# A hybrid encoder block on one Trainium2 core: a tenth gate and up pair of each FFN as a Strassen group, and half of each group's first sums made by an accumulating transfer

## The chip, the cores and the metric

The kernel runs on one core of one Trainium2 chip. The metric is device time in microseconds (us) of one execution. The engines named here are PE (TensorE, matrix products), DVE (VectorE), ACT (ScalarE), POOL (GpSimd, which here mostly issues transfers) and SP (SyncE, which issues the loads of raw weights).

## The reference, cut to what matters

One encoder block on 256 rows of width 2048, in float32: a half-step SwiGLU FFN, two token mixers (band attention and retention) whose outputs are gated and merged, a second FFN, and a final norm.

```
def swiglu_ffn(x, w_gate, w_up, w_down):          # 2048 -> 5632 -> 2048
    return (jax.nn.silu(x @ w_gate) * (x @ w_up)) @ w_down

x = x + 0.5 * swiglu_ffn(rmsnorm(x, norm_ffn1_g), ffn1_w_gate, ffn1_w_up, ffn1_w_down)
proj = rmsnorm(x, norm_mix_g) @ w_in              # q, k, v twice, three gates
...                                               # attention, retention
x = x + (sigmoid(gate_a) * (att @ w_out_att) + sigmoid(gate_r) * (ret @ w_out_ret)) @ w_out
x = x + 0.5 * swiglu_ffn(rmsnorm(x, norm_ffn2_g), ffn2_w_gate, ffn2_w_up, ffn2_w_down)
return rmsnorm(x, norm_final_g)
```

## The kernel before

**Products.** Every float32 product is made as three matmuls: weights and activations are split into a rounded part `hi` and the rest `lo`, and hi x hi, hi x lo and lo x hi are added up in PSUM (`three`, lines 131 to 133). A weight tile of 256 rows by 512 columns (512 KB) is split by one ACT cast (L123) and one DVE subtraction (L124) (`split`). Up to four split tiles exist at a time (`SPLIT_BUFS`), so splits run a few steps ahead of PE.

**Steps.** The whole program is one list of steps, and each step is one split tile and its products. A *standard* step loads its tile with an SP transfer into one of five raw buffers, and makes 12 matmuls (two 128-row tiles of rows, two chunks of K, three products). In this document it is written S.

**Strassen groups.** Gate and up of one 512-column block of an FFN (and pairs of columns of `w_in`) can be computed together as a 2 x 2 block product with seven instead of eight products (`class Strassen`). A group is named z with the number of its first step: z89 is the group that starts at step 89. It has 28 steps of 6 matmuls in four phases, each over four K chunks j = 0 to 3: r0 to r3 and s0 to s3 in phases 0, 1 and 2, and s0 to s3 alone in phase 3. Each group owns four tiles k (`kept`, loaded from up) and four tiles x (loaded from gate), which POOL loads (L507), in the order k0, x0, k1, x1, k2, x2, k3, x3. Then:
- Phase 0: r splits k. DVE adds k to x, the *first sum* (`first`, L496). s splits x.
- Phase 1: r splits a raw tile, which DVE then adds to x (L551). s splits x; then DVE makes k = x - k (L538), and POOL issues a transfer that adds a weight tile from DRAM to x, the *third sum* (`third`, L539).
- Phase 2: r splits a raw tile, s splits k. Phase 3: s splits x. After that the buffers go to later groups.

The order in which steps are prepared within a phase is r0 r1, s0 r2, s1 r3, s2 s3. In phase 0, r2's preparation holds the sum of x2, ahead of the split of s1.

**Order.** `weave` lays the groups one after another and puts standard steps between their pairs of steps. `SHARE` has one weight for each of the 16 pairs or single steps of a group; a credit grows by rate x weight, and when it is large enough, the next standard step of the queue is placed. A standard step of a down projection can only be placed when the blocks of its pass are at hand (`needs`, `makes`). `PLAIN` lists the blocks whose gate and up stay standard steps, and `PASSES` the groups of blocks that one pass over the down weights takes. Before, nine of the eleven blocks of each FFN are groups, and five more groups lie in the `w_in` product: 23 groups in all. POOL's queue holds the loads and third-sum transfers in the order of the program; the loads of the next group stand behind the third sums of the current one.

Of the kernel before, what the change touches and what calls it, by code (L numbers as in the profile page):

```python
# [11 lines left out]
ALU = mybir.AluOpType  # L12
# [28 lines left out]
RET_WAIT = (14, 5)  # L41
HELD = 6

SHARE = (0.85,) * 4 + (1.0,) * 4 + (0.8,) + (0.4,) * 3 + (0.15,) * 4
PLAIN = (9, 10)
PASSES = ((9, 0), (1, 2), (10, 3), (4, 5), (6,), (7,), (8,))
GATE_WAIT = 5
WARM = (6, 3)
TAIL_PARTS = ((0, slice(0, NB)), (1, slice(0, NB // 2)), (1, slice(NB // 2, NB)))

# [22 lines left out]
def block_kernel(ctx: ExitStack, tc: tile.TileContext, x, g1, w1g, w1u, w1d, gm, w_in, rel, woa, wor, wo,  # L73
                 g2, w2g, w2u, w2d, gf, cos, sin, decay, ident, out):
    nc = tc.nc
# [33 lines left out]
    def weights_tile(name):  # L109
        return wpool.tile([P, KC, NB], F32, tag="raw", bufs=RAW_BUFS, name=name)  # L110

    def chunk(w, r0, c0):
        return w[r0 : r0 + KC * P, c0 : c0 + NB].rearrange("(k p) n -> p k n", p=P)
# [367 lines left out]
    class Strassen:  # L481
# [20 lines left out]
        def loads(self):  # L502


            def go(tiles, i, jc):
                tiles[jc] = apool.tile([P, KC, NB], F32, tag="act", name=f"{self.name}{'kx'[i]}{jc}")
                nc.gpsimd.dma_start(tiles[jc], chunk(self.w[i], self.rows(0, jc), self.col[i]))  # L507

            return [
                lambda tiles=tiles, i=i, jc=jc: go(tiles, i, jc)  # L510
                for jc in range(HALF_K // KC) for i, tiles in enumerate((self.kept, self.x))
            ]
# [12 lines left out]
        def step(self, phase, jc, of_sum):  # L525
            made = {}
            name = f"{self.name}{phase}{jc}{'rs'[of_sum]}"
            n = HALF_K // KC

            def load():  # L530
                made["raw"] = weights_tile(f"raw{name}")
                i = 2 - phase
                fetch(made["raw"], self.w[i], self.rows(1, jc), self.col[i])

            def third():

                x, k = self.x[jc], self.kept[jc]
                nc.vector.tensor_sub(k, x, k)  # L538
                nc.gpsimd.dma_start(x, chunk(self.w[0], self.rows(1, jc), self.col[0]), accum_op=ALU.add)  # L539

            def prep():
                x = self.x[jc]
                if not of_sum:
                    if phase == 0:
                        made["w"] = split(self.kept[jc], name)
                        self.first(jc)
                        return
                    raw = made.pop("raw")
                    made["w"] = split(raw, name)
                    if phase == 1:  # L550
                        nc.vector.tensor_add(x, x, raw)  # L551
                elif phase == 2:
                    made["w"] = split(self.kept.pop(jc), name)
                elif phase == 3:
                    made["w"] = split(self.x.pop(jc), name)
                else:
                    made["w"] = split(x, name)
                    if phase == 1:
                        third()

            bank, form, fresh, closing = {
# [4 lines left out]
            }[phase, of_sum]  # L566

            def products():
                hi, lo = made["w"]
                if fresh and jc == 0:  # L570
                    self.bank(bank)
                for i in range(KC):
                    three(
                        self.acc[bank], self.norm.form(form, KC * jc + i), (hi[:, i, :], lo[:, i, :]),
                        fresh and jc == 0 and i == 0, closing and jc == n - 1 and i == KC - 1, True,
                    )
                if jc == n - 1:
                    self.end(phase, of_sum)

            loaded = not of_sum and phase in (1, 2)  # L580
            frees = ["raw"] if loaded else ["kept"] if of_sum and phase > 1 else []
            return Step(self, 0, load if loaded else None, prep, frees, products)
# [53 lines left out]
    def weave(jobs, apart, groups, lead, start=None):  # L636
# [18 lines left out]
        for _ in range(lead):  # L655
            next_standard()
        rate = (len(queue) - apart) / (len(groups) * sum(SHARE))
        credit = 0.0
        first = len(steps) - 8
        for n, (b, make) in enumerate(groups.items()):  # L660
# [5 lines left out]
            for i, part in enumerate(group.steps()):  # L666
                steps.extend(part)
                credit += rate * SHARE[i]
                if i + 1 == len(SHARE):
                    at_hand[b] = len(steps) + 6  # L670
# [5 lines left out]
    def ffn(name, norm, wg, wu, wd, after, start=None):  # L676


        nblocks = DFF // NB
        mids, ready = {}, {}  # L680

        def put_mid(b, hs):
            mids[b] = Operand(f"{name}a{b}", 1)
            for t in range(NT):
                mids[b].put(0, t, hs[t])

        def plain(b):
            gates = {}

            wait = GATE_WAIT if start is not None and b == PLAIN[0] else 0  # L690

            def gate_done(acc):
                def go():
                    for t in range(NT):
                        gates[t] = tmp_tile(f"{name}g{b}{t}", "gate", 2)
                        nc.scalar.activation(gates[t], acc[t], AF.Silu, scale=norm.scale(t))

                if wait:
                    later(wait, go)
                else:  # L700
                    go()

            def up_done(acc):
                for t in range(NT):
                    a = gates[t]
                    nc.vector.scalar_tensor_tensor(a, acc[t], norm.scale(t), a, op0=ALU.mult, op1=ALU.mult)  # L706
                later(3, lambda: put_mid(b, gates))

            tags = ("acc", "acc")
            up = Gemm(wu, 0, b * NB, D // P, norm, up_done, tags)  # L710
            up.makes = b
            return [Gemm(wg, 0, b * NB, D // P, norm, gate_done, ("z", "z") if wait else tags), up]

        def paired(b):
            got = {}

            def evict(t, side, r):
                if side == 1:
                    nc.scalar.activation(r, r, AF.Silu)
                    got[t] = r  # L720
                    return
                nc.vector.scalar_tensor_tensor(got[t], r, norm.scale(t), got[t], op0=ALU.mult, op1=ALU.mult)
                if t == 1:
                    later(3, lambda: put_mid(b, got))

            return Strassen(norm, wu, b * NB, wg, b * NB, evict)

        def down(blocks, last):

            jobs = []  # L730

            def act(k, t):
                return mids[blocks[k // 4]](k % 4, t)

            for b in range(D // NB):
                cols = slice(b * NB, (b + 1) * NB)

                def seed(acc, t, cols=cols):
                    nc.scalar.activation(acc, xs[t][:, cols], AF.Copy, scale=2.0)  # L739

                def evict(acc, t, cols=cols):
                    nc.scalar.activation(xs[t][:, cols], acc, AF.Copy, scale=0.5)  # L742

                if last:
                    job = Gemm(wd, 0, b * NB, 4 * len(blocks), act, down_done(b, 0.5, after))
                else:
                    job = Gemm(wd, 0, b * NB, 4 * len(blocks), act, None, ("acc", "acc"), seed)
                    job.evict = evict
                job.rows = [(m * 4 + i) * P for m in blocks for i in range(4)]
                job.needs = blocks  # L750
                jobs.append(job)
            return jobs

        downs = {blocks: down(blocks, blocks is PASSES[-1]) for blocks in PASSES}
        first, second = [plain(b) for b in PLAIN]
        order = [first, second[:1], downs[PASSES[0]], second[1:]] + [downs[p] for p in PASSES[1:]]
        jobs = [job for part in order for job in part]
        for job, follow in zip(jobs, jobs[1:]):
            job.next = follow
        groups = {b: (lambda b=b: paired(b)) for b in range(nblocks) if b not in PLAIN}  # L760
        weave(jobs, len(downs[PASSES[-1]]) * len(PASSES[-1]) * 4 // KC + HELD, groups, LEAD, start)

# [359 lines left out]

    warm_up(WARM[0])
    for s in steps:
# [19 lines left out]
    n1.put(0, 1)  # L1144
    warm_up(WARM[1])

# [85 lines left out]
```

## Time and profile before

| | |
|---|---|
| median of 3 runs | 2104.47 us (2101.32 to 2105.13) |
| profiled execution, time | 2103.97 us |
| profiled execution, span of instructions | 2102.2 us |
| PE / DVE / ACT / POOL busy | 98% / 84% / 67% / 13% |
| granted TensorE clock, mean | 0.998 |
| moved by DMA | 473.27 MB, 225 GB/s over the span |

In rows of groups and timelines, an instruction is named by line, engine, operation and output <- input, with tile names without their buffer numbers: `z89x` is any of the four x tiles of group z89, while `loz8912r` is the lo part of phase 1, chunk 2, row r of that group. In a list of waits the first name waited for the second; the numbers are the total, the count and the longest wait. A row of windows gives the stretch, then busy time of each engine, the granted clock, the mean busy share of the DMA engines, and GB/s. A share a little over 1 is a full engine.

### The profile page before, as it was taken

The numbers are of one execution on the slowest core, as the hardware profiler recorded it, in microseconds if no ns is written. First come the engines' busy times: TensorE is split into PE (matmuls) and PEld (weight loads), VectorE is DVE, ScalarE is ACT, GpSimd is POOL, SyncE is SP. The second block draws the span as 40 slices with busy tenths as digits, with TensorE's granted clock in tenths as the row PEclk, the third lists the DMA queues.
The fourth block names the chain that finished last, engine by engine and source line by source line (L and its number), as shares of the span: only waits on it lengthen the run. The fifth ranks groups of instructions, "written<-read, shape, count | busy, mean of one in ns | idle before, by whom it ended". The sixth has DMA issues, their size and how long they took to land.

```text
span 2102.2 us, 25815 instructions
## 1 busy us (share of the span) xinstructions
PE 2064.1 (98%) x9256; PEld 1687.6 (80%) x9256; DVE 1760.9 (84%) x1823; ACT 1407.8 (67%) x1734; POOL 274.0 (13%) x322
## 2 busy tenths in 40 slices
PE   9999999999999999999999999999999999999998
PEld 7788878878887888878788888887888788888886
DVE  7998889888997799889966667568889988898986
ACT  7677667767777766767664434556777677677785
POOL 1111211122111110122100000010122012110200
PEclk9999999999999999999999999999999999999999
DMA  8767886788668777788775645575788678866873
GB/s 302 210 214 229 261 229 198 233 253 253 192 227 247 241 209 235 256 280 250 217 256 178 220 131 191 189 245 167 229 271 238 184 228 261 245 195 225 277 210 130
DMA packets 219025, 473.27 MB, mean 225 GB/s; under 512 B 14784, under 2 KB 15536, under 8 KB 218896
## 3 DMA queue, kind: packets, MB, share of 16 engines
q1 hardware_dynamic: 161088, 310.42, 44.0%
q0 software_dynamic: 54752, 155.88, 27.4%
q10 hardware_dynamic: 3056, 5.32, 0.7%
q8 instruction: 72, 1.18, 0.2%
q14 instruction: 57, 0.47, 0.1%
HBM read 462.65 MB, written 8.91 MB: 224 GB/s over the span
## 4 chain that ended last, share of the span: by engine, by line
PE 76%; DVE 11%; issue 4%; ACT 4%; DMA 3%; POOL 0%; ACTq 0%; POOLq 0%; DVEq 0%
PE acc L132 15%; PE acc L133 14%; PE acc L131 14%; DVE lo L124 2%; DMA raw<-in_ffn_w_down_dram 2%; ACT hi L123 1%; DMA raw<-in_w_in_dram 1%; DMA rawz91523r<-in_ffn_w_up_dram 1%; DMA z992x<-in_ffn_w_gate_dram 1%; PE z128a L132 0%; PE z800a L132 0%; PE z380a L131 0%; PE z128a L131 0%; PE z800a L131 0%; PE z380a L133 0%
## 5 line engine op out<-in xcount | busy, mean ns | idle before, releaser
L124 DVE TENSOR_TENSOR lo<-raw,hi 128x1024 fp32r<-128x1024 f32 (+1 forms) x401 | 487.4, 1218 | 173.4 <-ACT hi L123 171.6
L123 ACT CAST hi<-raw 128x1024 fp32r<-128x1024 f32 (+1 forms) x401 | 419.0, 1048 | 231.3 <-PE acc L133 143.0
L739 ACT ACTIVATE acc<-xall 128x512 f32<-128x512 f32 x96 | 57.5, 599 | 8.4 <-DVE f1g L706 3.5
L742 ACT ACTIVATE xall<-acc 128x512 f32<-128x512 f32 x96 | 56.4, 588 | 4.6 <-PE acc L133 3.9
L131 PE MATMUL acc<-hi,mgh 128*128 128x512 f32 x128 | 50.1, 392 | 0.0
L133 PE MATMUL acc<-hi,mgl 128*128 128x512 f32 x128 | 49.8, 389 | 0.0
L132 PE MATMUL acc<-lo,mgh 128*128 128x512 f32 x128 | 49.8, 389 | 0.0
L132 PE MATMUL acc<-lo,nma01h 128*128 128x512 f32 x96 | 38.0, 396 | 2.7 <-DVE lo L124 2.7
L131 PE MATMUL acc<-hi,nma01h 128*128 128x512 f32 x96 | 38.6, 402 | 0.0
L131 PE MATMUL acc<-hi,nma00h 128*128 128x512 f32 x96 | 38.5, 401 | 0.0
L132 PE MATMUL acc<-lo,nma00h 128*128 128x512 f32 x96 | 37.9, 395 | 0.3 <-DVE lo L124 0.3
L133 PE MATMUL acc<-hi,nma01l 128*128 128x512 f32 x96 | 37.5, 391 | 0.0
L133 PE MATMUL acc<-hi,nma00l 128*128 128x512 f32 x96 | 37.5, 391 | 0.0
L131 PE MATMUL acc<-hi,nma10h 128*128 128x512 f32 x96 | 37.5, 390 | 0.0
L131 PE MATMUL acc<-hi,nma11h 128*128 128x512 f32 x96 | 37.4, 390 | 0.0
L133 PE MATMUL acc<-hi,nma11l 128*128 128x512 f32 x96 | 37.4, 390 | 0.0
L133 PE MATMUL acc<-hi,nma10l 128*128 128x512 f32 x96 | 37.4, 390 | 0.0
L132 PE MATMUL acc<-lo,nma10h 128*128 128x512 f32 x96 | 37.4, 389 | 0.0
L132 PE MATMUL acc<-lo,nma11h 128*128 128x512 f32 x96 | 37.4, 389 | 0.0
L133 PEld LDWEIGHTS acc<-hi,mgl 128*128 128x128 f32 x128 | 24.0, 188 | 4.9
L131 PEld LDWEIGHTS acc<-hi,mgh 128*128 128x128 f32 x128 | 24.0, 188 | 4.9
L132 PEld LDWEIGHTS acc<-lo,mgh 128*128 128x128 f32 x128 | 24.0, 188 | 4.9
(6130 smaller groups left out, 7143.7 us busy)
## 6 DMA issues: line engine op xcount, KB each, us to landing
raw<-in_ffn_w_down_dram SPq DMA_DIRECT2D x176, 512.0 KB, 6.3
raw<-in_w_in_dram SPq DMA_DIRECT2D x96, 512.0 KB, 4.5
raw<-in_ffn_w_up_dram SPq DMA_DIRECT2D x32, 512.0 KB, 9.8
raw<-in_w_out_dram SPq DMA_DIRECT2D x32, 512.0 KB, 3.7
raw<-in_ffn_w_gate_dram SPq DMA_DIRECT2D x31, 512.0 KB, 4.8
raw<-in_w_out_att_dram SPq DMA_DIRECT2D x16, 512.0 KB, 3.9
raw<-in_w_out_ret_dram SPq DMA_DIRECT2D x16, 512.0 KB, 4.1
z380x<-in_w_in_dram POOLq DMA_DIRECT2D x8, 512.0 KB, 8.0
```

The source lines that it names most:

```text
L123: nc.scalar.copy(hi[:, p, :], raw[:, p, :])
L124: nc.vector.tensor_sub(lo[:, p, :], raw[:, p, :], hi[:, p, :].bitcast(F32))
L131: nc.tensor.matmul(acc, ahi, whi, start=first, stop=False, **more)
L132: nc.tensor.matmul(acc, ahi, wlo, start=False, stop=False, **more)
L133: nc.tensor.matmul(acc, alo, whi, start=False, stop=last, **more)
L739: nc.scalar.activation(acc, xs[t][:, cols], AF.Copy, scale=2.0)
L742: nc.scalar.activation(xs[t][:, cols], acc, AF.Copy, scale=0.5)
```

## The change

Block 10 of both FFNs becomes a group too: 25 groups in all. The passes over the down weights are regrouped, and the weights in `SHARE` of the first two pairs of a group go from 0.85 to 0.5. For chunks 0 and 1 of each group (`BY_DMA = 2`) the first sum is no longer made by DVE: after the next load in the queue, POOL issues a second transfer of the same up tile that adds it to x in SBUF. The sums of chunks 2 and 3 stay on DVE.

```diff
-SHARE = (0.85,) * 4 + (1.0,) * 4 + (0.8,) + (0.4,) * 3 + (0.15,) * 4
-PLAIN = (9, 10)
-PASSES = ((9, 0), (1, 2), (10, 3), (4, 5), (6,), (7,), (8,))
+SHARE = (0.5,) * 2 + (0.85,) * 2 + (1.0,) * 4 + (0.8,) + (0.4,) * 3 + (0.15,) * 4
+PLAIN = (9,)
+PASSES = ((9, 0), (1, 2), (3, 4), (5, 6), (7,), (8,), (10,))
 GATE_WAIT = 5
+BY_DMA = 2
...
         def loads(self):
+            adds = []
+
             def go(tiles, i, jc):
                 tiles[jc] = apool.tile([P, KC, NB], F32, tag="act", name=f"{self.name}{'kx'[i]}{jc}")
                 nc.gpsimd.dma_start(tiles[jc], chunk(self.w[i], self.rows(0, jc), self.col[i]))
+                if adds:
+                    adds.pop()()
+                if i == 1 and jc < BY_DMA:
+                    adds.append(
+                        lambda: nc.gpsimd.dma_start(
+                            self.x[jc], chunk(self.w[0], self.rows(0, jc), self.col[0]), accum_op=ALU.add
+                        )
+                    )
...
                     if phase == 0:
                         made["w"] = split(self.kept[jc], name)
-                        self.first(jc)
+                        if jc >= BY_DMA:
+                            self.first(jc)
                         return
...
-        first, second = [plain(b) for b in PLAIN]
-        order = [first, second[:1], downs[PASSES[0]], second[1:]] + [downs[p] for p in PASSES[1:]]
+        order = [plain(b) for b in PLAIN] + [downs[p] for p in PASSES]
```

POOL's queue, before: the loads of group z128, behind the third sums of z89. In a name the tile's letter and chunk follow the group: `z128x0`.

```order
L507 DMA z128k0_2034<-in_ffn1_w_up_dram 128x2x512
L507 DMA z128x0_2080<-in_ffn1_w_gate_dram 128x2x512
L507 DMA z128k1_2104<-in_ffn1_w_up_dram 128x2x512
L507 DMA z128x1_2122<-in_ffn1_w_gate_dram 128x2x512
L507 DMA z128k2_2146<-in_ffn1_w_up_dram 128x2x512
L507 DMA z128x2_2158<-in_ffn1_w_gate_dram 128x2x512
L507 DMA z128k3_2173<-in_ffn1_w_up_dram 128x2x512
L507 DMA z128x3_2191<-in_ffn1_w_gate_dram 128x2x512
```

The same place of the changed program, where the group that starts as the fourth of the FFN is z116:

```order
L510 DMA z116k0_1874<-in_ffn1_w_up_dram 128x2x512
L510 DMA z116x0_1900<-in_ffn1_w_gate_dram 128x2x512
L510 DMA z116k1_1926<-in_ffn1_w_up_dram 128x2x512
L515 DMA z116x0_1900<-in_ffn1_w_up_dram 128x2x512
L510 DMA z116x1_1939<-in_ffn1_w_gate_dram 128x2x512
L510 DMA z116k2_1951<-in_ffn1_w_up_dram 128x2x512
L515 DMA z116x1_1939<-in_ffn1_w_up_dram 128x2x512
L510 DMA z116x2_1964<-in_ffn1_w_gate_dram 128x2x512
L510 DMA z116k3_1976<-in_ffn1_w_up_dram 128x2x512
L510 DMA z116x3_1991<-in_ffn1_w_gate_dram 128x2x512
```

The two accumulations (L515) stand between the loads, each behind the load that follows x0 or x1; each writes a tile that an earlier load of the same queue writes.

ACT, before: the end of phase 2 of z89, its phase 3, and the start of z128. The row of a standard step is `hi_...<-raw_...`; `hiz8930s` is phase 3, s0.

```order
L123 CAST hiz8922s<-z89k_1596 128x1024
L123 CAST hiz8923s<-z89k_1623 128x1024
L123 CAST hi_2130<-raw_2000 128x1024
L123 CAST hiz8930s<-z89x_1506 128x1024
L123 CAST hiz8931s<-z89x_1560 128x1024
L606 ACTIVATE z89c_2167<-z89a,n1minus 128x512
L123 CAST hiz8932s<-z89x_1609 128x1024
L123 CAST hiz8933s<-z89x_1641 128x1024
L123 CAST hi_2200<-raw_2014 128x1024
L719 ACTIVATE z89c_2167<-z89c_2167 128x512
L123 CAST hiz12800r<-z128k_2034 128x1024
```

The same place of the changed program, from z84 to z116:

```order
L124 CAST hiz8422s<-z84k_1465 128x1024
L124 CAST hiz8423s<-z84k_1511 128x1024
L124 CAST hiz8430s<-z84x_1374 128x1024
L124 CAST hiz8431s<-z84x_1435 128x1024
L124 CAST hiz8432s<-z84x_1493 128x1024
L618 ACTIVATE z84c_1985<-z84a,n1minus 128x512
L124 CAST hiz8433s<-z84x_1524 128x1024
L124 CAST hiz11600r<-z116k_1874 128x1024
L124 CAST hiz11601r<-z116k_1926 128x1024
L731 ACTIVATE z84c_1985<-z84c_1985 128x512
L124 CAST hiz11600s<-z116x_1900 128x1024
```

The two standard steps of this place are gone: their places in the queue moved into the next group.

## The prediction

> **What bounds the kernel now.** I read first the page's busy times and slices, then who waited for whom on TensorE (PE), then the order of time around one FFN group, z89, and the loading of the next, z128.
>
> ```profile
> span 2102.2 us, 25815 instructions
> PE 2064.1 (98%) x9256; PEld 1687.6 (80%) x9256; DVE 1760.9 (84%) x1823; ACT 1407.8 (67%) x1734; POOL 274.0 (13%) x322
> ...
> PE acc L132 <- DVE lo L124: 10.3, 21, 0.8
> ...
> PE z800a L131 <- ACT z800c L606: 0.8, 1, 0.8
> ```
>
> PE is busy 98% of the span, and its largest wait in total is 10.3 us. So PE's work sets the time, and VectorE (DVE, 84%) follows closely. The timeline gives the price of that work:
>
> ```profile
> 208.80 0.39 PE L131 MATMUL acc<-hi,f1a9h 128*128 128x512 f32 x1
> ...
> 211.52 0.39 PE L131 MATMUL z89a<-hiz8910s,n1s6h 128*128 128x512 f32 x1
> ...
> 264.43 0.39 PE L131 MATMUL z128c<-hiz12801s,n1s5h 128*128 128x512 f32 x1
> ```
>
> Between the first two rows lies one standard step, 12 matmuls: 2.72 us, or 0.2267 us each (the 0.39 is latency; matmuls overlap). A Strassen step of 6 takes 1.36 us. From the second row to the third lie 228 matmuls and 8 transposes: 52.91 us, of which 51.7 are the 228 and 1.2 the rest. PE hardly waits in this stretch.
>
> DVE and the DMA engines are busier than their averages in part of each group:
>
> ```profile
> 209.47 1.22 DVE L538 TENSOR_TENSOR z89k<-z89x,z89k 128x1024 f32<-128x1024 f32 x1
> ...
> 215.15 1.22 DVE L538 TENSOR_TENSOR z89k<-z89x,z89k 128x1024 f32<-128x1024 f32 x1
> ...
> 231.03 0.74 DVE L598 SCALAR_TENSOR_TENSOR z89c<-z89c,n1minus,z89c 128x512 f32<-128x512 f32 x1
> ```
> ```profile
> core 0: us, PE busy (x) PEld busy (x) DVE busy (x) ACT busy (x) POOL busy (x), PEclk, DMA share, GB/s
> 202.00:214.00 12.00, 12.00 (x54) 9.95 (x53) 11.70 (x11) 9.89 (x13) 1.24 (x1) 1.00 0.62 181
> 214.00:254.00 40.00, 40.00 (x177) 32.73 (x176) 34.53 (x32) 26.24 (x29) 9.45 (x11) 1.00 1.03 322
> 254.00:278.00 24.00, 24.00 (x110) 19.53 (x109) 23.42 (x23) 16.43 (x18) 0.00 (x0) 1.00 0.34 101
> ```
>
> Five DVE operations start in 5.68 us, 1.136 us each, without a pause. The DMA engines are full (share 1.03) for 40 us of the group, and two-thirds idle after it. The transfers that the next group needs are issued in the full part, by GpSimd (POOL):
>
> ```profile
> 211.23 1.24 POOL L539 DMA_DIRECT2D z89x<-in_ffn_w_up_dram  x1 [30.75 <-DVE z89k L538]
> ...
> 224.84 1.19 POOL L539 DMA_DIRECT2D z89x<-in_ffn_w_up_dram  x1 [1.08 <-issue]
> 225.57 1.23 POOL L507 DMA_DIRECT2D z128k<-in_ffn_w_up_dram  x1
> 226.32 1.23 POOL L507 DMA_DIRECT2D z128x<-in_ffn_w_gate_dram  x1
> ...
> 236.43 0.72 POOL L507 DMA_DIRECT2D z128x<-in_ffn_w_gate_dram  x1 [4.29 <-DVE loz8921s L124]
> ```
>
> POOL issues in order, and a transfer that has to wait holds those behind it (30.75 us before the first row). Now the times to landing: the four accumulating transfers of z89 (L539), then k0 and x0 of z128 (rows 225.57 and 226.32), then k0 and x0 of z684, issued into an emptier queue.
>
> ```profile
> DMA to landing us min/median/max: 5.9/5.9/9.3
> ...
> DMA to landing us min/median/max: 10.7/10.7/10.7
> ...
> DMA to landing us min/median/max: 12.0/12.0/12.0
> ...
> DMA to landing us min/median/max: 4.3/4.3/4.3
> ...
> DMA to landing us min/median/max: 4.9/4.9/4.9
> ```
>
> **The change, part by part.**
>
> *Matmuls.* A plain pair is 16 standard steps, 192 matmuls; a group is 28 Strassen steps, 168. Block 10 of both FFNs becomes a group: 2 x 24 x 0.2267 = 10.9 us off PE, which bounds. Nothing hides that gain.
>
> *DVE and ACT.* The groups grow from 23 to 25. First sums on DVE go from 92 (23 x 4) to 50 (25 x 2): 42 less. The two groups add 24 splits and 16 other sums: 40 more. At 1.136 us that is -48 and +45 us: no change in total. ScalarE gets 24 casts and 8 evictions more at 67% busy. Both lie beside PE, so I cost them at nothing, except where DVE is the later one (below).
>
> *Standard steps.* With `PLAIN = (9,)` only 104 instead of 120 standard steps per FFN are woven into ten groups instead of nine, and the first passes wait for blocks 0, 2, 4 and 6, one group each. The written order shows what comes of it: standard steps stand in bunches. z84 has none in its phases 2 and 3; z116 then has six there. In each FFN four joints are thin (z12 to z44, z84 to z116, z156 to z188, z227 to z260). From phase 1's s0 to the next group's s1 they hold 144 matmuls (the first two) or 156, where z89 to z128 held 228. All other joints keep 204 to 242.
>
> *The bank wait.* Where no standard step stands between phases 2 and 3, PE waits for ScalarE's copy of bank a: 0.8 us in the row of z800. There are 5 such places now and 9 after: 4 x 0.8 = +3.2 us.
>
> *The accumulating transfers.* In POOL's order the transfer for x0 stands behind k1, and waits for x0's load to land. Behind it stand x1 and k2; then x1's accumulation waits for x1; behind that x2, k3, x3. So the three x loads, which were issued independently, become a chain. At the thin joints I follow it from t = 0, the issue of phase 1's first third-sum transfer (211.23 in z89):
> - The last third-sum transfer came 13.6 us later; with one standard step less (1.14 us of DVE) it comes at 12.5. x0 is issued 1.5 us behind it, as at 226.32: 14.0.
> - With a full queue: x0 lands 12.0 later (26.0). The accumulation is issued at 26.5 and lands 5.9 later (32.4), and x1 2.1 behind it (34.5; k0 and x0 of z128 landed so far apart, at 236.3 and 238.3). The second one is issued at 35.0 and lands at 40.9, x2 at 43.0.
> - With an empty queue: x0 at 18.9, x1 at 26.6, x2 at 34.3 (4.9 for a load, 5.9 for an accumulation, 1.3 between two landings: issues 0.7 apart, and 4.9 against 4.3).
> - In phase 0 DVE adds k2 to x2 before it splits x1 for s1. So s1 is ready two operations, 2.3 us, and a signal of 0.2 us after x2: at 36.8 to 45.5.
>
> PE begins s0 at 0.3 (211.52) and would reach s1 after 144 x 0.2267 + 1.2 = 33.8 us, at 34.1; with 156 matmuls at 36.9, where the chain too is 1.1 later. The stall is therefore 2.7 to 11.4 us at the first kind of joint and 1.0 to 9.7 at the second. I take 5.5 and 3.9, below the middle: no raw load of a standard step competes in phases 2 and 3 there, so the queue is emptier than z128's. Eight joints: 4 x 5.5 + 4 x 3.9 = +37.6 us. At the other joints PE reaches s1 at 46.5 or later, and the full-queue chain (one more operation before it) is ready at 46.6: no wait worth counting.
>
> The Trainium skill (DMA: Bandwidth & Descriptors, section on the anatomy of one DMA) says that DMA engines do not wait on semaphores; the issuing sequencer waits before it dispatches. The 30.75 us ahead of the first L539 row agree: the queue behind it stood still. Were the wait kept inside the DMA engines, x1 and x2 would be issued as now, and the sum would be rival A's.
>
> The sum against the profiled execution (2103.97 us, half a microsecond under the median of 2104.47): -10.9 + 3.2 + 37.6 = +29.9, so 2133.9; beside the median 2134.4. I forecast **2134 us**.
>
> **Rivals.**
>
> *A, faster: the transfers are hidden.* If x2 lands before 34.1 - 2.5 = 31.6 us, no joint waits for it. For it: the accumulations of z89 landed in 5.9 us even at share 1.03. Against it: even the empty-queue chain takes 34.3. DVE alone has 29 operations and four small ones between, 29 x 1.136 + 4 x 0.7 - 0.6 = 35.1 us, 1.2 over PE at the 144-matmul joints. If leads absorb that, -10.9 + 3.2 gives 2096.8; with some of the 10.3 us of waits for DVE gone too, 2094.
> The same page of the Trainium skill fits a transfer as 2.0 us plus its bytes at 436 GB/s. For 512 KB that makes 3.2 us, and by that estimate x2 would land at about 27, and A would hold; the trace has 4.9 and 12.0 for a load, and decides.
>
> *B, no difference: queue nearly empty.* Stalls between DVE's own 1.2 and the empty queue's 2.7 us make 5 to 15 us in all, and cancel the gain: 2102 to 2112.
>
> *C, slower still: the waits cost clock.* At the end of the kernel PE stops at 2091.8:
>
> ```profile
> 2092.00:2094.00 2.00, 0.00 (x0) 0.00 (x0) 1.67 (x5) 1.54 (x4) 0.70 (x1) 1.00 0.00 0
> 2094.00:2096.00 2.00, 0.00 (x0) 0.00 (x0) 0.75 (x1) 1.53 (x3) 0.29 (x1) 0.70 0.80 307
> 2096.00:2098.00 2.00, 0.00 (x0) 0.00 (x0) 0.00 (x0) 0.00 (x0) 0.00 (x0) 0.50 1.04 349
> ...
> 2.77 1.48 PE L1121 MATMUL pswz<-warm 128*128 128x512 f32 x3
> ```
>
> The clock falls to 0.50 about 3 us later, and the last row shows three matmuls before the clock is up in 1.48 us: 0.2 us slower each. If every long stall is followed by some 8 such matmuls, that adds 8 x 1.6 = 13 us: 2147.
> The Trainium skill (TensorE: Matmul & The Clock Gate, on the two states) puts that fall after an idle window of about 3.4 us; the windows above agree. What speaks against it is that a stall may come in pieces shorter than 3 us.
>
> *D, the queue is full everywhere.* With 9.3 us for each accumulation the chain grows by 6.8 us. Thin joints then stall by up to 18, and joints of 204 to 218 matmuls begin to wait as well: 2165 and more.
>
> **How the numbers follow.** Forecast 0.44 (2112 to 2145), C 0.10, D 0.10, B 0.14, A 0.22. A range of 2094 to 2166 takes in A's end, the full-queue values up to 9.5 and 7.9 us a joint (-10.9 + 3.2 + 70 = +62), and leaves most of D out. The forecast's own range is 2112 to 2145. A measurement here tells 0.2%, 4.2 us, from no change: faster 0.22 (A); same 0.11 (most of B); slower 0.67 (the others and B's end).
>
> **What would show it.** About 48 matmuls fewer on PE, at 0.227 us. On POOL, ahead of the new accumulations, idle time ended by the landing of x loads. On PE and DVE, waits of 3 to 6 us for DVE sums x2 and splits of s1 at z44, z116, z188 and z260 and their twins of the second FFN, and none at z156 or in w_in's groups. The granted clock near those joints decides C. The prediction is wrong if x2's sum at z116 starts without a wait, or if the thin joints are stopped by something else than the chain of x loads.

## The result, and the profile after

| | before | after |
|---|---|---|
| median of 4 runs, us | 2102.99 | 2238.11 (2231.62 to 2239.15) |
| ratio | | 1.0635 (95%: 1.0612 to 1.0659) |
| span of the profiled execution, us | 2102.2 | 2236.9 |
| granted clock, mean | 0.998 | 0.975 |

The change costs 6.4%. The direction and the main place were forecast; the size was not. Two rows near the head of the page after, the busy times and PE's slices:

```profile
PE 2095.9 (94%) x9208; PEld 1699.2 (76%) x9208; DVE 1765.2 (79%) x1825; ACT 1436.8 (64%) x1766; POOL 359.0 (16%) x396
...
PE   9989898998999999999999999999898988989998
```

PE makes 48 matmuls fewer (9208), as counted, but is busy 94% instead of 98% of a longer span. The slices with an 8 lie in the two FFNs, and the last one at the kernel's end; `w_in` and the mixers in the middle show none. The list of PE's waits after shows what took the place of the 0.8 us rows:

```profile
PE acc L133 <- DVE lo L125: 24.0, 30, 5.3
PE f2a4p L351 <- DVE z840c L734: 8.9, 1, 8.9
PE f1a6p L351 <- DVE z227c L734: 8.5, 1, 8.5
...
PE f1a2p L351 <- DVE z84c L734: 5.6, 1, 5.6
...
PE z84a L132 <- ACT z84c L618: 0.8, 1, 0.8
```

There are eight waits of 5.6 to 8.9 us, one at each thin joint, 60.0 us in all. PE stands before the transposes (L351) of the last block's product: they need DVE's operation L734, and L734 needs nothing that is late. It stands in DVE's queue behind a first sum. DVE, at the joint from z84 to z116:

```profile
247.28 1.23 DVE L125 TENSOR_TENSOR loz11600s<-z116x,hiz11600s 128x1024 fp32r<-128x1024 f32 x1 [3.21 <-ACT hiz11600s L124]
...
255.02 1.23 DVE L497 TENSOR_TENSOR z116x<-z116x,z116k 128x1024 f32<-128x1024 f32 x1 [3.86 <-DMA z116x<-in_ffn_w_gate_dram]
256.16 0.75 DVE L734 SCALAR_TENSOR_TENSOR z84c<-z84a,n1rstd,z84c 128x512 f32<-128x512 f32 x1
256.82 1.22 DVE L125 TENSOR_TENSOR loz11601s<-z116x,hiz11601s 128x1024 fp32r<-128x1024 f32 x1
```

The sum of x2 (third chunk) waits 3.86 us for x2's load, and L734 and the split of s1 wait behind it. The load was late because of POOL's queue, of which these are the rows from the first third-sum transfer of z84 to the load of x2; the last row is the time to landing of x0's load, issued at 226.79:

```profile
212.36 1.24 POOL L550 DMA_DIRECT2D z84x<-in_ffn_w_up_dram  x1 [29.07 <-ACT hiz8411s L124]
...
225.31 1.22 POOL L550 DMA_DIRECT2D z84x<-in_ffn_w_up_dram  x1 [1.54 <-ACT hiz8420s L124]
226.04 1.25 POOL L510 DMA_DIRECT2D z116k<-in_ffn_w_up_dram  x1
226.79 1.26 POOL L510 DMA_DIRECT2D z116x<-in_ffn_w_gate_dram  x1
227.53 1.24 POOL L510 DMA_DIRECT2D z116k<-in_ffn_w_up_dram  x1
239.96 1.24 POOL L515 DMA_DIRECT2D z116x<-in_ffn_w_up_dram  x1 [11.19 <-DMA z116x<-in_ffn_w_gate_dram]
240.71 1.23 POOL L510 DMA_DIRECT2D z116x<-in_ffn_w_gate_dram  x1
...
247.74 1.23 POOL L515 DMA_DIRECT2D z116x<-in_ffn_w_up_dram  x1 [5.07 <-DMA z116x<-in_ffn_w_gate_dram]
248.50 1.22 POOL L510 DMA_DIRECT2D z116x<-in_ffn_w_gate_dram  x1
```
```profile
DMA to landing us min/median/max: 12.9/12.9/12.9
```

This is the chain of the prediction, link by link: behind x0's issue two idle stretches of POOL, 11.19 and 5.07 us, each ended by the landing of an x load. Counted from 212.36, as the prediction counts:

| us from the first third-sum transfer | forecast, full queue | measured |
|---|---|---|
| x0 issued | 14.0 | 14.4 |
| first accumulation issued | 26.5 | 27.6 |
| second accumulation issued | 35.0 | 35.4 |
| x2 landed (its sum starts) | 43.0 | 42.7 |
| split of s1 ready | 45.5 | 45.7 |

The full-queue end of the forecast came true to within about a microsecond. I had taken a value nearer to the empty queue.

For a cost per joint I take the time from phase 1's s0 of one group to that of the next, and subtract 0.2267 us for each matmul and 0.15 for each transpose; the rest is called *lost*. The windows of the joint from z84 to z116 and of the next, which is not thin:

```profile
213.36:277.92 64.56, 55.28 (x226) 43.70 (x224) 52.28 (x49) 39.40 (x44) 13.25 (x15) 0.89 0.77 211
277.92:348.52 70.60, 69.90 (x309) 56.91 (x308) 59.07 (x55) 51.30 (x59) 12.20 (x14) 1.00 0.82 241
```

The first has 216 matmuls and 8 transposes, 50.2 us, and takes 64.56: 14.4 lost. The second has 300 and 8, 69.2 us, and takes 70.60: 1.4 lost. Over all such stretches but that of the mixers 28.0 us are lost before (21 stretches) and 169.6 after (23): 116.4 at the eight thin joints (13.4 to 15.8 each) and 53.2 at the other 15. So 141.6 more are lost, 10.9 saved by the 48 matmuls, and some 4 us lie elsewhere; that is the 134.7 us between the spans.

The clock falls too. Four windows of 2 us, at the wait and behind it:

```profile
250.00:252.00 2.00, 1.40 (x6) 0.79 (x4) 1.16 (x1) 0.00 (x0) 1.17 (x2) 0.50 0.98 157
252.00:254.00 2.00, 0.00 (x0) 0.00 (x0) 0.00 (x0) 0.26 (x1) 0.00 (x0) 0.50 1.07 310
256.00:258.00 2.00, 1.04 (x5) 1.04 (x6) 2.00 (x4) 1.55 (x2) 0.00 (x0) 0.50 0.47 172
264.00:266.00 2.00, 2.00 (x11) 1.65 (x10) 1.23 (x1) 1.71 (x3) 0.00 (x0) 1.00 0.24 91
```

The granted clock is at 0.50 before the long wait of 5.57 us begins (at about 251.4): shorter pauses of PE came first. It is still 0.50 when PE has work again, and full at 264. The clock records add up to 79 us at 0.50 at the eight thin joints.

### The profile page after: what moved, and what is told of

It is laid out like the page before. It is cut to its first block, busy times and chain, and to the rows that moved or that the text cites. A ratio compares the mean times of both kernels' runs of the same rounds, so it can differ in the third digit from the quotient of the medians.

```text
span 2236.9 us, 25894 instructions
## 1 busy us (share of the span) xinstructions
PE 2095.9 (94%) x9208; PEld 1699.2 (76%) x9208; DVE 1765.2 (79%) x1825; ACT 1436.8 (64%) x1766; POOL 359.0 (16%) x396
## 3 DMA queue, kind: packets, MB, share of 16 engines
q0 software_dynamic: 72832, 194.69, 34.7%
## 4 chain that ended last, share of the span: by engine, by line
PE 36%; DMA 11%; DVE 10%; issue 9%; ACT 3%; POOL 2%; ACTq 0%; POOLq 0%; DVEq 0%
PE acc L133 8%; PE acc L134 8%; PE acc L132 8%; DMA raw<-in_ffn_w_down_dram 2%; DVE lo L125 2%; DMA z728x<-in_ffn_w_gate_dram 1%; ACT hi L124 1%; DMA z944x<-in_ffn_w_gate_dram 1%; DMA z430x<-in_w_in_dram 1%; DMA z392x<-in_w_in_dram 1%; DMA z800x<-in_ffn_w_gate_dram 1%; DMA z872x<-in_ffn_w_gate_dram 1%; DMA raw<-in_w_in_dram 0%; DMA z467x<-in_w_in_dram 0%; DMA z467k<-in_w_in_dram 0%
## 5 line engine op out<-in xcount | busy, mean ns | idle before, releaser
L125 DVE TENSOR_TENSOR lo<-raw,hi 128x1024 fp32r<-128x1024 f32 (+1 forms) x369 | 448.7, 1219 | 189.8 <-ACT hi L124 188.4
L124 ACT CAST hi<-raw 128x1024 fp32r<-128x1024 f32 (+1 forms) x369 | 385.3, 1048 | 237.0 <-PE acc L134 147.5
L133 PE MATMUL acc<-lo,nma10h 128*128 128x512 f32 x96 | 37.6, 392 | 0.0
L134 PE MATMUL acc<-hi,nma10l 128*128 128x512 f32 x96 | 37.6, 391 | 0.0
```

The source lines that it names most:

```text
L124: nc.scalar.copy(hi[:, p, :], raw[:, p, :])
L125: nc.vector.tensor_sub(lo[:, p, :], raw[:, p, :], hi[:, p, :].bitcast(F32))
L133: nc.tensor.matmul(acc, ahi, wlo, start=False, stop=False, **more)
L134: nc.tensor.matmul(acc, alo, whi, start=False, stop=last, **more)
```

## The experiments

My theory after the result: the thin joints pay for the chain of POOL's waits, through a queue of the DMA engines that is full there. Rivals: the fallen clock is the price; the accumulating packets fill the DMA engines and so make everything late; the bunched standard steps are to blame, or the tenth group itself.

**All first sums back on DVE.** Ten groups, bunched as in the change, and no second transfers.

```diff
-BY_DMA = 2
+BY_DMA = 0
```


> The changed kernel with all first sums on DVE again (BY_DMA = 0); ten groups, passes and SHARE as changed. Theory (the chain of x loads behind the accumulating transfers makes PE wait at the thin joints, and the waits cost clock): loads are issued without a wait again, x2 lands about 35 us after the first third sum instead of 42.6, and DVE with two more sums is ready at about 37.5 against PE's 34.1: 3 to 4 us lost at each of the eight thin joints instead of 14.5, no half clock; 2110 to 2130 us. Rival 1 (thin joints stall by themselves, for want of standard steps): over 10 us lost at each, 2180 us or more. Rival 2 (the accumulations' DMA time fills the queue everywhere): 2100 to 2130, no different from the theory.

Measured: 2154.61 us, ratio 1.0246 (1.0205 to 1.0288). The second transfers thus cost 83 us, net of the 50 sums that go back to DVE. But 51 us over the kernel before remain, more than the theory's 2110 to 2130, and the thin joints lose 4.0 to 7.5 each instead of 3 to 4. A thin joint (z84 to z116) and the next show why:

```profile
206.57:260.78 54.21, 51.27 (x225) 41.01 (x224) 53.53 (x51) 39.37 (x44) 10.31 (x13) 1.00 0.78 231
260.78:334.00 73.22, 70.17 (x309) 56.86 (x308) 61.37 (x57) 50.80 (x59) 10.10 (x12) 1.00 0.71 220
```

In the thin joint DVE is busy 53.53 of 54.21 us: it is the bound there, and the joint still loses 4.0.

**Nine groups, with second transfers.** The kernel before, with the new code of the loads and `BY_DMA = 2`, and nothing else.

```diff
+BY_DMA = 2
...                                   # loads() and the condition on first() as in the change
```


> The kernel before with only the accumulating transfers added (BY_DMA = 2; nine groups, old passes and SHARE). Theory: no joint is thin (284 to 308 matmuls a group), the chain ends about 43 to 47 us after the first third sum and PE needs 47 to 53, so a group loses 0 to 3 us: 2100 to 2125 us, no window at half clock after the first group. Rival 1: 2095 to 2105. Rival 2 (DMA time of the accumulations): the groups lose 3 us or more everywhere, 2150 us or more.

Measured: 2130.23 us, ratio 1.0130 (1.0100 to 1.0161). Even where the joints hold 228 matmuls and where no group was added, the transfers cost 27 us, net of the 46 sums that DVE no longer makes. That is more than the theory had (2125 at most) and less than the 2150 of rival 2.

**Nine groups, both x loads ahead.** The same, but the queue issues x0 and x1 first and accumulates only behind k2: x0 x1 k0 k1 k2, both accumulations, x2 k3 x3.

```diff
+                if (i, jc) == (0, BY_DMA):
+                    while adds:
+                        adds.pop(0)()
...
+            order = [(jc, 1, self.x) for jc in range(BY_DMA)] + [(jc, 0, self.kept) for jc in range(BY_DMA)]
+            order += [(jc, i, t) for jc in range(BY_DMA, n) for i, t in enumerate((self.kept, self.x))]
```


> The kernel before (nine groups) with the accumulating transfers, in the same new queue order. Theory: the loop of about 60 us is shorter than every group (66 to 69 us), so the accumulations cost nothing, and the DVE sums that they take over save up to 10 us of waits: 2092 to 2106 us. Rival (DMA time): 2115 to 2135, as with the old queue order (2130).

Measured: 2102.77 us, ratio 1.0000 (0.9989 to 1.0011). POOL at the joint from z89 to z128, first with the changed code (nine groups), then with x0 and x1 ahead:

```profile
225.19 1.25 POOL L510 DMA_DIRECT2D z128x<-in_ffn_w_gate_dram  x1
...
237.83 1.23 POOL L515 DMA_DIRECT2D z128x<-in_ffn_w_up_dram  x1 [10.31 <-DMA z128x<-in_ffn_w_gate_dram]
...
249.21 1.23 POOL L515 DMA_DIRECT2D z128x<-in_ffn_w_up_dram  x1 [8.68 <-DMA z128x<-in_ffn_w_gate_dram]
249.96 1.22 POOL L510 DMA_DIRECT2D z128x<-in_ffn_w_gate_dram  x1
```
```profile
225.29 2.00 POOL L510 DMA_DIRECT2D z128x<-in_ffn_w_gate_dram  x2
...
236.46 1.23 POOL L516 DMA_DIRECT2D z128x<-in_ffn_w_up_dram  x1 [5.07 <-DMA z128x<-in_ffn_w_gate_dram]
238.38 1.21 POOL L516 DMA_DIRECT2D z128x<-in_ffn_w_up_dram  x1 [0.70 <-DMA z128x<-in_ffn_w_gate_dram]
239.13 1.24 POOL L510 DMA_DIRECT2D z128x<-in_ffn_w_gate_dram  x1
```

Both make the same transfers. With x0 and x1 in flight together the second wait shrinks from 8.68 to 0.70 us, and x2 is issued at 239.13 instead of 249.96. That order alone is worth the 27 us. It brings no gain over the kernel before, though, because PE is the bound there (98% busy in both) and DVE, which has 46 sums less, is not.

**Ten groups, x loads not held.** The changed kernel with both accumulations behind x2's load: k0 x0 k1 x1 k2 x2, accumulation, k3, accumulation, x3.

```diff
-                if adds:
-                    adds.pop()()
+                if (i, jc) in ((1, BY_DMA), (0, BY_DMA + 1)) and adds:
+                    adds.pop(0)()
```


> The changed kernel with the two accumulating transfers issued later in POOL's queue: k0 x0 k1 x1 k2 x2, sum of x0, k3, sum of x1, x3. Same transfers and bytes, but x1 and x2 no longer wait behind a landing. Theory: x2 lands some 10 us earlier; what is left is x1's sum and x3, 3 to 6 us late; a thin joint loses 4 to 8 us, little of it at half clock: 2130 to 2170 us. Rivals 1 and 2: no better than 2200 us, since neither the standard steps nor the DMA work change.

Measured: 2186.69 us, ratio 1.0399 (1.0369 to 1.0429): 51 us below the changed kernel, so neither rival holds, but above the 2130 to 2170 that I expected. The thin joints fall from 13.4 to 15.8 us lost to 9.0 to 10.6, not to 4 to 8. The wait has moved from x2 to x0, as the row of PE at z116's s0 and the landing of x0's accumulation (issued 236.60) show:

```profile
PE z116c L132 <- ACT hiz11600s L124: 4.8, 1, 4.8
```
```profile
DMA to landing us min/median/max: 9.0/9.0/9.0
```

x0 is now the last to be whole: its load, POOL's wait for it, and 9.0 us of a second transfer that shares the queue with the loads issued ahead of it.

**Plain instead of accumulating.** The changed kernel, with the second transfers not adding.

```diff
-   self.x[jc], chunk(self.w[0], self.rows(0, jc), self.col[0]), accum_op=ALU.add
+   self.x[jc], chunk(self.w[0], self.rows(0, jc), self.col[0])
```


> The changed kernel, with the second transfer of x0 and x1 made a plain one that overwrites x (the gate's part of chunks 0 and 1 is left out of the result). Each transfer still waits for its load to land, and the queue behind it stands as before; what falls is the work of the DMA engines in those transfers. Theory (the time goes into the waits for landings in POOL's order, one after the other): the eight thin joints still lose 10 to 13 us each, 2190 to 2220 us. Rival (the accumulating packets keep the DMA engines full, and that makes the landings late): the loads land in 5 to 8 us, thin joints lose 4 to 7.5 as without the second transfers, at most 2165 us.

Measured: 2178.60 us, ratio 1.0368 (1.0352 to 1.0383), between the two theories' numbers. POOL at the same joint as above, and the time to landing of x0's load:

```profile
220.13 1.23 POOL L510 DMA_DIRECT2D z116x<-in_ffn_w_gate_dram  x1
...
233.33 0.73 POOL L515 DMA_DIRECT2D z116x<-in_ffn_w_up_dram  x1 [11.24 <-DMA z116x<-in_ffn_w_gate_dram]
...
240.73 0.72 POOL L515 DMA_DIRECT2D z116x<-in_ffn_w_up_dram  x1 [4.92 <-DMA z116x<-in_ffn_w_gate_dram]
```
```profile
DMA to landing us min/median/max: 12.9/12.9/12.9
```

POOL's waits (11.24 and 4.92) and x0's landing (12.9) are those of the changed kernel: the accumulations do not make the chain. They lengthen it a little (x1's load lands 6.1 us after issue here, 6.7 there), and x0 is whole later (its second transfer lands in 4.1 us here, 6.1 there). The thin joints lose 8.9 to 11.7, 82 us in all; with accumulating transfers it was 116, with all sums on DVE 41. So at these joints the plain transfers with their waits take some 40 us and the accumulation another 35. Over the whole kernel the accumulation is the larger part, 60 of the 83 us. Both theories hold a part.

**Half clock.** The changed kernel, with 24 matmuls of which nothing is used put behind the first s0 of the eight groups after a thin joint, to keep PE awake.

```diff
+                if (phase, of_sum, jc) == (0, True, 0) and self.name in FILL_AT:
+                    idle = side_tile(f"idle{self.name}")
+                    for _ in range(FILL):
+                        nc.tensor.matmul(idle, self.norm.form(form, 0)[0], hi[:, 0, :], start=True, stop=True)
```


> The changed kernel with 24 matmuls that nobody reads (5.4 us of PE work) placed behind the first s0 of the eight groups after the thin joints, in the time in which PE waits. If the half clock after the wait costs time, as this theory has it, PE no longer stands still long enough to lose its clock there: half-clock time at the eight joints near 0 instead of 79 us, 2 to 3 us less lost at each, 2212 to 2225 us. Rival: the half clock is covered, because what follows waits for the chain of x loads anyway: 2232 to 2245 us in spite of the full clock.

Measured: 2228.65 us (2224.15 to 2233.16), ratio 1.0594 (1.0540 to 1.0647). That lies between the two theories. The half clock at the thin joints falls from 79 to 24 us, and 192 matmuls, 43.5 us of PE, find room without making the kernel longer. The medians differ by 9 us, and the intervals of the two ratios overlap; in the two traces the eight joints take 11 us less. So the clock is a small part of what the joints cost. How small stays open, since 24 us at half clock are left and the added matmuls can themselves delay what stands behind them.

**An even spread.** A cap on `weave`'s credit keeps the standard steps from bunching. It was run four ways: with the changed kernel's queue, with the sums on DVE, with x0 and x1 ahead, and with both accumulations behind x2.

```diff
-                credit += rate * SHARE[i]
+                credit = min(credit + rate * SHARE[i], 1.2)
```


> The changed kernel with the credit for standard steps capped at 1.2, so that they don't bunch: every group from the second on has 7 or 8 standard steps, every joint about 5; the chain of transfers is as in the change. Theory: PE reaches s1 at about 45 us and the chain is ready at 45 to 47: 1 to 4 us lost at each joint, half clock rare; 2105 to 2145 us. Rival 1 (thin joints alone): 2090 to 2105. Rival 2 (DMA time): 2180 us or more.

> The capped credit (standard steps spread evenly) and all first sums on DVE: neither thin joints nor a chain. Theory (a group can't be shorter than the loop from its third sums through the loads to the next third sums, 64 to 70 us with the chain, and without it no shorter than DVE's work, 48 operations at 1.136 us and some 4 us): PE's 58 to 61 us just cover DVE's 58, so 1 to 3 us are lost in a group: 2110 to 2140 us. Rival (the uneven spread did no harm without the chain): the same as with DVE sums and bunched steps, 2150 to 2158.

> The changed kernel with even standard steps and POOL's queue in another order: x0 x1 k0 k1 k2, sum of x0, sum of x1, x2 k3 x3. x0 and x1 land while others are issued, and one wait of some 4 us stands in the queue instead of two of 10 to 12 us together with 7. Theory: the loop shortens by about 8 us to some 58 to 60 us, which PE's 58 to 61 us cover; DVE has 46 operations, 56 us: 0 to 2 us lost in a group, 2092 to 2120 us, no half clock. Rival (accumulations cost DMA time whatever their place): 4 us or more lost in each group, 2160 us or more.

> The changed kernel with standard steps spread evenly over the groups and both accumulating transfers queued behind x2's load, so that no x load waits for another's landing. Theory (the chain of waits is the price, and what the transfers cost beside it is small): between 2105 and 2131 us, no slower than the even spread with all first sums on DVE (2131), since DVE has two sums less per group. Rival (the accumulating transfers' own DMA time makes x2 and the raw tiles late): 2140 to 2175 us.

| first sums of chunks 0, 1 | time, us | ratio (95%) | lost over all groups |
|---|---|---|---|
| transfers, queue as in the change | 2247.27 | 1.0687 (1.0646 to 1.0728) | 176.4 |
| DVE | 2131.35 | 1.0131 (1.0102 to 1.0160) | 66.4 |
| transfers, x0 and x1 ahead | 2162.30 | 1.0278 (1.0232 to 1.0324) | 93.5 |
| transfers, behind x2 | 2162.57 | 1.0285 (1.0268 to 1.0302) | 96.8 |

The first row was my worst miss: I had expected the even spread to take most of the loss away, and it made the time no better. The group from z80 to z115 shows what I had not seen, and so does PE's list, where twelve waits of 5.1 to 7.4 us end with L734, as they do at the thin joints. The group, and the longest of these waits:

```profile
203.13:272.65 69.52, 63.79 (x273) 51.69 (x272) 58.26 (x55) 45.90 (x52) 13.79 (x15) 0.95 0.78 226
```
```profile
PE f1a6p L351 <- DVE z222c L734: 7.4, 1, 7.4
```

The group holds 61.0 us of PE work and takes 69.52, nearly as long as groups that hold 69.2. My reading is that the chain closes on itself: third sums, x0's load, its landing, x1, its landing, x2, phase 0, phase 1, the next third sums. With the changed queue and ten groups, bunched or even, every group takes 63 us or more, whether its PE work is 50 or 61. A group of 66 to 72 us of work nearly hides that loop (0.6 to 2.2 us lost in the FFNs of the changed kernel); ten groups share fewer standard steps, and whether a few groups of 50 or all of 58 to 61 lie under it makes little difference. No run measures the loop by itself; what speaks for it is that the same steps and transfers in a better queue shorten these groups (z80 to z115 takes 63.85 us with both accumulations behind x2).

The second row fell in its theory's range. The two better queues both take 85 us off the first row, and both end above what the theory gave them: against DVE's sums they are still 31 us slower, so here the rivals' numbers hold. The two rows of windows are groups z80 to z294 with the sums on DVE, and the same with both accumulations behind x2:

```profile
192.08:569.62 377.54, 365.72 (x1610) 295.82 (x1608) 351.93 (x324) 271.16 (x310) 64.21 (x72) 1.00 0.76 231
```
```profile
195.16:580.88 385.72, 369.54 (x1609) 295.32 (x1608) 339.84 (x312) 268.59 (x310) 78.92 (x84) 1.00 0.83 243
```

DVE has 12 us less to do (351.93 to 339.84) and the stretch takes 8 us more, while the DMA share rises from 0.76 to 0.83. Here no x load waits for another. What is left shows in the waits of the last of these runs: ACT's splits of s0 and s1 wait for the second transfers to land (4.8 us at z728), and PE's waits for the splits of s steps make 23 us in all, where they make 6 with the sums on DVE. The runs do not split this between the transfers' own work and POOL's waits ahead of them.

**One transfer instead of two, even spread, behind x2.**

```diff
-BY_DMA = 2
+BY_DMA = 1
...
+                if (i, jc) == (1, 2) and adds:
+                    adds.pop(0)()
```


> The changed kernel with standard steps spread evenly, one accumulating transfer per group in place of two, queued behind x2's load. Theory: the even spread without such transfers lost 1.6 to 3.7 us per group to DVE; one sum less (1.14 us) in 25 groups takes off up to 28 us: 2103 to 2122 us. Rival (POOL's wait for x0's landing makes k3 and x3 late, or the DMA time counts): 2131 us or more.

Measured: 2143.75 us, ratio 1.0199 (1.0184 to 1.0214), in the rival's range: 12 us worse than none and 19 better than two. With an even spread each such transfer costs more than the DVE sum that it saves.

**Nobody makes the sums.** What would ten groups bring if the sums cost nothing? The even spread, with neither sum nor transfer for chunks 0 and 1.

> Ten groups with standard steps spread evenly, and the first sums of chunks 0 and 1 made by nobody: neither by VectorE nor by a second transfer (they are left out of the result). VectorE has the 50 sums less that the change takes off it, and the queue is that of the kernel before. Theory (with ten groups in even spread VectorE's work is what costs the 28 us against nine groups, 2131 against 2103): 50 sums of 1.14 us off lets the matmuls' 10.9 us show, 2092 to 2105 us. Rival (the shorter groups lose to something else: loads that come later than the shorter group needs them, or the joints' own waits): 2115 to 2131 us.

Measured: 2097.09 us, ratio 0.9970 (0.9958 to 0.9982). The same groups, z80 to z294:

```profile
188.00:555.63 367.63, 364.37 (x1610) 296.28 (x1608) 339.06 (x312) 271.35 (x310) 64.23 (x72) 1.00 0.78 237
```

With 12.9 us less DVE work than with all sums on DVE, the stretch is 9.9 us shorter (367.63 against 377.54). The theory's number held: DVE's work is what keeps ten evenly spread groups at 2131, and ten groups pay, by 6 us, if half of the first sums are free. No version that makes all the sums beat the kernel before.

## Why the prediction was right or wrong

- **Matmuls, -10.9 us: right.** 48 fewer, and the kernel that leaves out half of the sums shows 6 us of the gain.
- **Bank wait, +3.2 us: right.** The list has nine such waits, eight of 0.8 and one of 1.1 us.
- **DVE and ACT in total, nothing: right for the total, wrong for the cost.** DVE's total moved by 4 us (1760.9 to 1765.2). But ten groups take less PE time per group and nearly the same DVE time, so DVE comes close to PE within a group. With all sums on DVE ten groups ended 28 us (even) to 51 us (bunched) above the kernel before. I looked at the total, and let DVE count only where the chain made it late.
- **The chain: right as a mechanism, and link by link in time.** The eight places are exactly the eight forecast, but PE stops earlier than I said: not at s1, but at the transposes that stand ahead of it, because L734 is queued on DVE behind the sum of x2. Before that it already stands for up to 2.3 us at s0, whose split waits for x0's accumulation. My own times had that wait (x0 whole at 32.4, PE at s0 at about 30), and I did not count it.
- **The stall at a thin joint, taken as 5.5 and 3.9 us: this is the step that failed.** They lost 13.4 to 15.8 each (0.8 of it the bank wait), 116.4 in all where 37.6 were forecast, and the time of 2238 us lies beyond the range's end of 2166. My reason for the low value was that "no raw load of a standard step competes in phases 2 and 3 there". SP's rows at the joint say otherwise:

```profile
219.78 6.05 SPq L118 DMA_DIRECT2D raw<-in_ffn_w_down_dram  x2
226.59 0.37 SPq L118 DMA_DIRECT2D rawz11610r<-in_ffn_w_gate_dram  x1
228.87 0.37 SPq L118 DMA_DIRECT2D rawz11611r<-in_ffn_w_gate_dram  x1
231.79 0.37 SPq L118 DMA_DIRECT2D raw<-in_ffn_w_down_dram  x1
```
```profile
224.00:240.00 16.00, 15.22 (x66) 11.98 (x66) 15.33 (x15) 12.99 (x15) 3.50 (x5) 1.00 1.05 298
```

  A raw load is issued when a buffer is free, not when its step is near. Where no standard step uses a buffer, SP loads ahead for the bunch behind the joint and for phase 1 of the next group. From 224 to 240 the packets of SP's loads take 41.8% of the DMA engines' time and those of POOL's transfers 63.1%; in the same stretch before, at z89, it was 36.5% and 68.9%. So the queue was as full as at z128 (share 1.05), x0 landed in 12.9 us, and the upper end of my range per joint was nearer to the truth than the value I took. No run takes these loads away; that they kept the queue full is read from the rows and shares.
- **Rival C, the clock: it happened, at all eight joints, and accounts for a part of what they lose beyond the upper end of 11.4.** At z116 the s1 matmuls start at 260.44, 48.1 us after the first third-sum transfer, although their split is there at 45.7. Ahead of them lie the late transposes and six matmuls at 0.43 us each instead of 0.23, which make some 1.4 of these 2.4 us. PE's rows of that place, from s0 on:

```profile
247.30 0.49 PE L132 MATMUL z116c<-hiz11600s,n1s5h 128*128 128x512 f32 x1 [1.57 <-ACT hiz11600s L124]
...
256.96 1.11 PE L351 MATMUL f1a2p<-id_sb,z84c 128*128 128x128 f32 x4 [5.57 <-DVE z84c L734]
257.73 0.77 PE L132 MATMUL z116a<-hiz11602r,n1a00h 128*128 128x512 f32 x1
258.30 0.63 PE L133 MATMUL z116a<-loz11602r,n1a00h 128*128 128x512 f32 x1
258.73 0.63 PE L134 MATMUL z116a<-hiz11602r,n1a00l 128*128 128x512 f32 x1
...
260.44 0.63 PE L132 MATMUL z116c<-hiz11601s,n1s5h 128*128 128x512 f32 x1
```

  I had priced it at 13 us, as a rival with 0.10. At the eight joints 75 matmuls start while the clock is at 0.50, and at 0.2 us each that makes 15 us; the run with the added matmuls took 11 us off these joints.
- **Other joints, "no wait worth counting": wrong.** The 15 stretches lose 53.2 us where all 21 before lost 28.0, above all z299, z505 and z983 (6.8 to 8.3 each), which hold 61 to 63 us of PE work, less than the loop takes, and z335 (9.0). I had followed the chain from third sum to s1 only, and not on to the next third sum. "None in w_in's groups" fails with them (z392 loses 4.6).
- **Rivals A, B, D.** A and B fell with x2 at 42.7 instead of 31.6 us. D (2165 and more) had waits at other joints too, but its mechanism did not come: the accumulations landed in 6.1 us, not 9.3.

The rule that I cited from the Trainium skill (DMA: Bandwidth & Descriptors, anatomy of one DMA), that the issuing sequencer waits and not the DMA engines, agrees with POOL's 11.19 us; its fit of 2.0 us plus bytes at 436 GB/s, by which I had estimated 3.2 us for 512 KB, does not hold where the share is 1.05: the load took 12.9.

## What to carry to other kernels

A transfer that depends on an earlier one of the same in-order queue turns the loads behind it into a chain: put every independent load ahead of the first dependent transfer (here that order alone was worth 27 us at equal work). Price the dependent transfer itself as well: with an even spread it cost more than the DVE sum that it saved, in all four runs that had it. Follow such a chain all the way round to its own start; if the loop is longer than a group's compute, every shorter group can be stretched towards it, however the work is spread. And when a prefetching queue fills gaps by itself, an empty stretch in the program is no sign of an empty DMA queue.

## What the runs showed of the hardware

- An accumulating 512 KB transfer costs more DMA time than a plain one: in the changed kernel's joint it landed in 6.1 us, the plain one at the same place in 4.1, the packets of POOL's queue take 34.7% of 2236.9 us with accumulating transfers and 32.3% of 2176.6 us with plain ones, which is 73 us less, or 1.5 us a transfer; and 50 transfers made plain took 60 us off the kernel (2238 to 2179).
- With the DMA engines full, a 512 KB load took 12.9 us to land whether or not the second transfers behind it accumulated.
- After a wait the clock stayed at 0.50 for several us of work: it came back between 262 and 264, 5 to 7 us after PE had begun to work again at 256.96.
